# Modulation vectors made during the two layers: products on the vector engine, sums over the partitions on the tensor engine

## The chip, the cores and the metric

The kernel runs on one core of one Trainium2 chip. The metric is device time in microseconds (us) of one execution, as the median of several runs. The engines that matter here are TensorE (PE in the profile, its weight loads PEld), VectorE (DVE), ScalarE (ACT), GpSimd (POOL) and SyncE (SP), which issues the DMAs that load weights.

## What is computed

Two blocks of a network on 512 latent tokens and 256 context tokens, 1024 features, float32. The first block has two attention layers. Each layer is modulated by vectors that are products of a conditioning vector with a weight matrix; so is each layer of the second block:

```python
def layer(x, cx, c_silu, cctx_silu, norm_w, ada_w, ada_b, ..., need_ctx):
    mod = c_silu @ ada_w + ada_b                  # [3 * 1024]
    mod_c = cctx_silu @ ada_w + ada_b
    shift, scale, gate = jnp.split(mod, 3, axis=-1)
    shift_c, scale_c, gate_c = jnp.split(mod_c, 3, axis=-1)
    hx = rmsnorm(x, norm_w) * (1 + scale[:, None, :]) + shift[:, None, :]
    hc = rmsnorm(cx, norm_w) * (1 + scale_c) + shift_c
    ...                                           # projections, three attentions, output projection
    x = x + gate[:, None, :] * (ux @ w_out)

def _adaln(cvec, w_mod, b_mod, n_chunks):         # second block, six vectors of 1024 per layer
    m = jax.nn.silu(cvec) @ w_mod[:, :n_chunks * D_MODEL] + b_mod[:n_chunks * D_MODEL]
    return [m[:, None, j * D_MODEL:(j + 1) * D_MODEL] for j in range(n_chunks)]
```

The second layer of the first block has no further use for the context tokens, so it needs no gate for them. The second block needs the context's vectors only for the first two of its first layer's six chunks.

## The kernel before

The program is written with a scheduling library: the Python code issues instructions in one order, and a scheduler sorts them for each engine by priority and readiness; each engine then works through its own queue in that order. Stages follow one another. In a first phase (up to about 181 us in the profile) the modulation vectors of layer 0, the filters and the context's recurrence are made. Then come the two layers, `layer(0, ...)` and `layer(1, ...)`, up to about 1600 us; then the second block with a mixer, an expert mixture, a conformer and another expert mixture.

In a layer the projections (`proj_tok`, `proj_feat`) load 256 columns of weights with two tiles of a ring (`wload`, L123; tiles of 4 KB per partition, four in the ring during the layers), split them into two parts on ScalarE (L153) and GpSimd (L154), and multiply them with the tokens in three products each (L159 to L161 or L327 to L329). Attention works on pairs of heads between them: row maxima on VectorE (L671 to L692), transposed scores and products with v on TensorE (L721, L724, L727), exponentials on ScalarE (L777). In the layers PSUM's eight banks are divided as m=2, s=2, av=1, b=3, and any other kind, such as "a", takes from b.

At the end of each projection `self.fill(1)` (L331, L356) runs one unit of a generator, `self.filler`, set up at L400 to L404. Its units make modulation vectors that are needed later: 12 units for layer 1 of the first block (3 x 1024 columns of `ada_w[1]`), 16 for chunks 2 to 5 of the second block's first layer, and 12 for chunks 0 to 2 of its second. A unit's instructions get the same priorities as the code that follows it (`background`, L164).

A unit of `adaln` (L191) takes 256 columns: two ring tiles of weights [128, 4, 256], then eight matmuls (L205) with a stationary of 32 columns, 128 rows each, in which the two vectors silu(c) and silu(c_ctx) stand at a unit's own column pair and the rest is zero, and 256 moving weight columns. Four of them share TensorE's columns at a time. A matmul in float32 has two records in the profile. VectorE then adds the product to a tile of rows (`adr`, L208, L210). After every twelve units (or the last) two matmuls with the selection matrix `sel` (L215) sum and transpose the rows, and VectorE adds the bias (L218). The zero-padded vectors `z1` and `z2` come from `cvec` (L178), at the start of the first block. The first phase uses `adaln` for layer 0's vectors and the first eight groups of `w_mod[0]`, the conformer for the last twelve of `w_mod[1]` (L1555).

Of the kernel before, what the change touches and what calls it, by code (L numbers as in the profile page):

```python
# [43 lines left out]
def kview(src):  # L44
    """[k * 128, n] of DRAM as [128, k, n]."""
    return src.rearrange("(k p) n -> p k n", p=128)


class K:
# [20 lines left out]
    def chunks(self, pool, tag, n, width, dt=F32, bufs=None):  # L70
        """n tiles of their own, so that each waits only for what held its place."""
        return [self.t(pool, [128, width], dt, tag=f"{tag}{i}", bufs=bufs) for i in range(n)]

    @contextmanager
    def banks(self, **caps):
        """A phase's division of the eight PSUM banks among kinds of use; any other kind takes from b."""
# [35 lines left out]
    # ------------------------------------------------------------------ streamed weights  # L112
# [10 lines left out]
    def wload(self, src, nk, n, tag="ring", size=1024, bufs=None):  # L123
        """Weights [128, nk, n], loaded through 4 KB tiles of the ring; w(k, m) is a view of chunks k..k+m."""
# [17 lines left out]
    def split(self, src):  # L142
        """Exact two-part float32r split of src ([128, <= 512] elements)."""
# [20 lines left out]
    def background(self, offset=0):  # L164
        """Instructions that give way to those of the code that follows."""
# [11 lines left out]
    # ------------------------------------------------------------------ modulation vectors  # L177
    def cvec(self, pool, name):  # L178
        """Zero-padded stationary columns of silu(c), silu(c_ctx)."""
# [9 lines left out]
        return z  # L189

    def adaln(self, z, wsrc, ncols, bias, mod, tmp, part=None):  # L191
        """mod[128, ncols / 128, 2] = (silu(c), silu(c_ctx)) @ w + b with features on partitions; a
        generator of units, one 256-column group each.  Row 2g + v of a group's product is vector v."""
# [31 lines left out]
    # ------------------------------------------------------------------ norms  # L225
# [3 lines left out]
    def sums(self, n, tmp, square=True, sc=None, kind="q", four=True, alloc=None):  # L229
        """Sums over the features: add(k, x) takes chunk k as soon as it is there (four: four of them share the  # L230
        tensor engine); add() gives four partial sums of 32 equal rows each, SBUF [128, n]."""
# [34 lines left out]
    def rsqrt(self, tmp, x):  # L266
        """1 / sqrt(x) for x > 0, [128, <= 24], by Newton's method from an estimate out of the exponent."""
# [10 lines left out]
    def tokmean(self, s, n, tmp):  # L278
        """Means per token, tokens on partitions: [128, n / 128] in PSUM."""
# [5 lines left out]
    def spread(self, r, n):  # L285
        """[128 tokens, n / 128] to [128 rows, n tokens], every row the same; in PSUM."""
# [1696 lines left out]
```

## Time and profile before

| what | us |
|---|---|
| median of 3 runs | 3200.13 |
| lowest and highest | 3197.77, 3202.67 |
| span of the profiled execution, first to last instruction | 3197.7 |
| PE busy | 2936.5 (92%) |
| DVE busy | 1390.3 (43%) |
| ACT busy | 932.1 (29%) |
| POOL busy | 782.0 (24%) |

The profiled execution's time and its span can be taken as one; it lies 2.4 us below the median of the runs. Busy time is the union of an engine's instructions; matmuls overlap in the pipeline, so that the mean duration of one times the count is more than the busy time. "The chain of waits" is the chain of work that ended last, followed back from the last instruction to what released it at each step; a line's share of it is time that the end waited for. "issue" is time in which an engine waited for nothing that the profile shows. A fraction such as 0.98 for PEclk is the granted clock of TensorE, the mean over a window of its two levels (2.4 GHz, and half of that).

### The profile page before, as it was taken

The page shows a single profiled execution, that of the slowest core. Times are in us where ns is not written, and L with a number is a line of the kernel's source. Part 1 is how long each engine was busy: PE and PEld are TensorE (multiplying, and loading weights), DVE is VectorE, ACT ScalarE, POOL GpSimd, SP SyncE. Part 2 cuts the span into 40 slices and gives each one's busy share as a digit, 9 for nine tenths or more (in the row PEclk, how much of TensorE's full clock was granted, in tenths as well). Part 3 has the DMA queues.
Part 4 walks back from the last instruction along what each step waited for, and adds up shares of the span by engine and source line. Part 5 has one row for each costly group of instructions (what it writes and reads, how often), then busy time and mean ns, then how long its engine had stood idle before and what let it go on. Part 6 is the DMA issues. An engine that isn't in the chain of part 4 may idle for free.

```text
span 3197.7 us, 39095 instructions
## 1 busy us (share of the span) xinstructions
PE 2936.5 (92%) x15406; PEld 1837.9 (57%) x15406; DVE 1390.3 (43%) x2645; ACT 932.1 (29%) x1667; POOL 782.0 (24%) x669
## 2 busy tenths in 40 slices
PE   6899999999898999999998779999899998899988
PEld 3485567765677566755775664444444664444443
DVE  5765553455405543675267761111215552211122
ACT  3434543354313444343345220100012231001001
POOL 2233232322423333343444640000002430000000
PEclk8999999999999999999999889999999998999999
DMA  9631133211533133322331268999993567999993
GB/s 286 198 113 34 34 122 110 79 63 43 171 99 113 47 99 116 123 65 94 112 97 60 92 261 344 385 391 401 399 362 90 163 228 282 393 387 394 397 404 122
DMA packets 302599, 621.36 MB, mean 194 GB/s; under 512 B 15215, under 2 KB 185207, under 8 KB 302160
## 3 DMA queue, kind: packets, MB, share of 16 engines
q1 hardware_dynamic: 294240, 597.63, 51.4%
q0 software_dynamic: 4848, 17.04, 1.7%
q10 hardware_dynamic: 3328, 4.20, 0.4%
q8 instruction: 121, 1.98, 0.2%
q14 instruction: 62, 0.51, 0.1%
HBM read 603.96 MB, written 14.95 MB: 194 GB/s over the span
## 4 chain that ended last, share of the span: by engine, by line
PE 77%; DVE 13%; ACT 3%; issue 3%; POOL 2%; DMA 2%; SPq 0%; DVEq 0%; ACTq 0%; POOLq 0%
PE b L1793 22%; PE b L159 8%; PE b L160 7%; PE b L161 7%; PE av L727 5%; PE b L1744 5%; PE b L205 3%; PE s L721 3%; DVE xn L1772 2%; PE s L724 2%; PE m L702 1%; PE b L329 1%; PE b L328 1%; PE b L327 1%; PE b L1771 1%
## 5 line engine op out<-in xcount | busy, mean ns | idle before, releaser
L154 POOL TENSOR_TENSOR wl<-ring,wh 128x512 fp32r<-128x512 f32 x304 | 404.4, 1333 | 715.7 <-ACT wh L153 702.8
L1793 PE MATMUL b<-mr,xs 128*64 128x512 f32 x1920 | 441.2, 604 | 0.0
L153 ACT CAST wh<-ring 128x512 fp32r<-128x512 f32 x304 | 186.8, 618 | 548.8 <-PE b L161 393.4
L159 PE MATMUL b<-hh,wh 128*128 128x512 f32 (+1 forms) x800 | 293.2, 367 | 2.4 <-DVE sc L585 1.1
L160 PE MATMUL b<-hh,wl 128*128 128x512 f32 (+1 forms) x800 | 290.3, 363 | 1.3 <-POOL wl L154 1.3
L161 PE MATMUL b<-hl,wh 128*128 128x512 f32 (+1 forms) x800 | 288.7, 362 | 0.1
L1793 PEld LDWEIGHTS b<-mr,xs 128*64 128x64 f32 x1920 | 143.4, 139 | 225.2 <-issue 215.3
L1793 PE MATMUL b<-mq,xs 128*64 128x512 f32 x1152 | 260.8, 599 | 0.0
L1744 PEld LDWEIGHTS b<-G,kt 128*128 128x128 f32 x1024 | 137.7, 211 | 136.1 <-issue 80.6
L1744 PE MATMUL b<-G,kt 128*128 128x128 f32 x1024 | 160.2, 308 | 52.0 <-DVE G L1736 52.0
L727 PE MATMUL av<-P,kv 128*64 128x512 f32 (+2 forms) x672 | 187.2, 514 | 2.8 <-ACT P L777 1.8
L159 PEld LDWEIGHTS b<-hh,wh 128*128 128x128 f32 x800 | 151.7, 190 | 37.4 <-issue 8.2
L160 PEld LDWEIGHTS b<-hh,wl 128*128 128x128 f32 x800 | 152.3, 190 | 30.9 <-issue 8.7
L161 PEld LDWEIGHTS b<-hl,wh 128*128 128x128 f32 x800 | 151.5, 189 | 29.0 <-issue 8.4
L1749 DVE TENSOR_SCALAR xs<-b,s1m,m 128x128 f32<-128x128 f32 x64 | 26.2, 410 | 322.2 <-PE b L1744 322.2
L1793 PEld LDWEIGHTS b<-mq,xs 128*64 128x64 f32 x1152 | 85.9, 137 | 138.2 <-issue 133.2
L777 ACT ACTIVATE P<-s 128x512 f32<-128x512 f32 (+2 forms) x224 | 116.9, 550 | 114.2 <-PE s L724 111.0
L327 PE MATMUL b<-wh,hh 128*128 128x256 f32 x512 | 147.8, 289 | 2.3 <-DVE kb L1124 1.3
L329 PE MATMUL b<-wh,hl 128*128 128x256 f32 x512 | 147.5, 289 | 1.1 <-DVE hl L310 0.9
L328 PE MATMUL b<-wl,hh 128*128 128x256 f32 x512 | 147.4, 288 | 0.3 <-POOL wl L154 0.3
L1747 ACT ACTIVATE xs<-b,m,s1m 128x128 f32<-128x128 f32 x64 | 29.3, 457 | 373.4 <-PE b L1744 373.4
L1553 POOL TENSOR_SCALAR dg<-ident,vec 128x128 f32<-128x128 f32 x5 | 2.9, 595 | 537.1 <-PE b L1793 537.1
(536 smaller groups left out, 5588.0 us busy)
## 6 DMA issues: line engine op xcount, KB each, us to landing
mr<-in_exp_w_dram SPq DMA_DIRECT2D x240, 1024.0 KB, 9.7
mq<-in_exp_w_dram SPq DMA_DIRECT2D x144, 1024.0 KB, 11.5
ring<-in_w_mod_dram SPq DMA_DIRECT2D x96, 512.0 KB, 4.0
ring<-in_w_in_dram SPq DMA_DIRECT2D x96, 512.0 KB, 3.5
ring<-in_ada_w_dram SPq DMA_DIRECT2D x48, 512.0 KB, 3.6
ring<-in_w_out_dram SPq DMA_DIRECT2D x32, 512.0 KB, 4.1
bias<-in_BS_dram POOLq DMA_DIRECT2D x16, 512.0 KB, 4.0
bias<-in_BT_dram POOLq DMA_DIRECT2D x16, 512.0 KB, 4.1
```

The lines of the kernel that those rows point to most:

```text
L153: nc.scalar.copy(h, src)
L154: nc.gpsimd.tensor_tensor(l, src, h.bitcast(F32), op=ALU.subtract)
L159: m(out, w[0], x[0], start=start, stop=False, skip_group_check=chk)
L160: m(out, w[1], x[0], start=False, stop=False, skip_group_check=chk)
L161: m(out, w[0], x[1], start=False, stop=stop, skip_group_check=chk)
L327: m(o, hh, wh[:, kk, :], start=(k == 0 and i % 2 == 0), stop=False, skip_group_check=True)
L328: m(o, hh, wl[:, kk, :], start=False, stop=False, skip_group_check=True)
L329: m(o, hl, wh[:, kk, :], start=False, stop=stop, skip_group_check=True)
L727: mm(av[64 * i:64 * i + 64, a:b], vf(i, kt), P, start=start, stop=stop)
L777: nc.scalar.activation(p[:, :w], ps[:, :w], AF.Exp)
L1744: mm(px, kt[t][:, c * 128:c * 128 + 128], G[:, t, :], start=t == 0, stop=t == 3)
L1793: mm(ps[hf][64 * e:64 * e + 64, :], lhs(k, e), wt[e][:, k2, hf * 512:hf * 512 + 512], start=k == 0, stop=k == 7)
```

## The change

`adaln_v` takes the place of `adaln` in the filler of the two layers. The product runs on VectorE: a tile of weights [128 rows, n columns] is multiplied by one number per partition, silu(c) of that row, and added to a running sum `acc` (tag `adr`, [128, 1024], one buffer). With both vectors (`nv=2`) n is 512 and a group has 16 such operations in two units; with one vector (`nv=1`) n is 1024 and a group has 8 operations in four units. At a group's end eight matmuls sum over the partitions: 128 columns of `acc` are the stationary operand, two columns of ones are moving. Then VectorE adds the bias. The number of units, the ring tiles per unit and the bytes loaded stay the same; the rows that a load fetches are 512 or 1024 elements long in place of 256. Vectors that are not used (the context's gate of layer 1, the context's part in the second block's later chunks) are no longer made.

`cvec` also returns the vectors without padding, kept in the pool of the first block, and the padded ones move to a pool of the first phase; the two calls come after the loads of sink, rope and bsel. The first phase and the conformer keep `adaln`. Comments and docstrings are dropped throughout, which shifts line numbers only.

```diff
-    def cvec(self, pool, name):
+    def cvec(self, pool, name, keep=None):
...
-        return z
+        if keep is None:
+            return z
+        s = self.t(keep, [128, 8, 2], tag=name + "s")
+        nc.vector.tensor_copy(s[:], z[:, :, 32:34])
+        return z, s
...
+    def adaln_v(self, z, wsrc, a, b, nv, bias, mod, tmp):
+        nc = self.nc
+        n = 1024 // nv
+        for c0 in range(a, b, n):
+            acc = self.t(tmp, [128, 1024], tag="adr", bufs=1)[:].rearrange("p (v n) -> p v n", v=nv)
+            for k0 in range(0, 8, 2 * nv):
+                w = self.wload(kview(wsrc[k0 * 128:(k0 + 2 * nv) * 128, c0:c0 + n]), 2 * nv, n)
+                for k in range(2 * nv):
+                    for v in range(nv):
+                        x = z[:, k0 + k, v:v + 1]
+                        if k0 + k == 0:
+                            nc.vector.tensor_scalar(acc[:, v, :], w(k), x, None, op0=ALU.mult)
+                        else:
+                            nc.vector.scalar_tensor_tensor(acc[:, v, :], w(k), x, acc[:, v, :], op0=ALU.mult, op1=ALU.add)
+                if k0 + 2 * nv < 8:
+                    yield 1
+            ps = self.bank("a")
+            m = n // 128
+            for c in range(m):
+                for v in range(nv):
+                    o = 2 * (nv * c + v)
+                    nc.tensor.matmul(ps[:, o:o + 2], acc[:, v, c * 128:c * 128 + 128], self.one32[:, 0:2], start=True, stop=True)
+            c0 //= 128
+            nc.vector.tensor_tensor(
+                mod[:, c0:c0 + m, 0:nv], ps[:, 0:2 * nv * m].rearrange("p (c v two) -> p c v two", v=nv, two=2)[:, :, :, 0],
+                bias[:, c0:c0 + m][:, :, None].to_broadcast([128, m, nv]), op=ALU.add)
+            yield 1
...
-            z1 = self.cvec(fp, "cv1")
-            z2 = self.cvec(fp, "cv2")
             self.sink = load("sink", [128, 2, 8])
...
                 with self.pool("fl") as fl, self.pool("ec") as ec:
+                    z1, c1 = self.cvec(ec, "cv1", fp)
+                    z2, c2 = self.cvec(ec, "cv2", fp)
...
             def units():
-                yield from self.adaln(z1, A["ada_w"][1], 3 * D, self.v("ada_b1"), self.mods[1], fp)
-                yield from self.adaln(z2, A["w_mod"][0], 6 * D, self.v("b_mod0"), self.m2[0], fp, (8, 24))
-                yield from self.adaln(z2, A["w_mod"][1], 6 * D, self.v("b_mod1"), self.m2[1], fp, (0, 12))
+                yield from self.adaln_v(c1, A["ada_w"][1], 0, 2 * D, 2, self.v("ada_b1"), self.mods[1], fp)
+                yield from self.adaln_v(c1, A["ada_w"][1], 2 * D, 3 * D, 1, self.v("ada_b1"), self.mods[1], fp)
+                yield from self.adaln_v(c2, A["w_mod"][0], 2 * D, 6 * D, 1, self.v("b_mod0"), self.m2[0], fp)
+                yield from self.adaln_v(c2, A["w_mod"][1], 0, 3 * D, 1, self.v("b_mod1"), self.m2[1], fp)
```

## Rows read from the trace of the kernel before

**Rows 1.** Busy time by engine in the layers' stretch, with its header.

```profile
core 0: us, PE busy (x) PEld busy (x) DVE busy (x) ACT busy (x) POOL busy (x), PEclk, DMA share, GB/s
181.00:1600.00 1419.00, 1367.06 (x7656) 950.74 (x7654) 698.09 (x1411) 562.17 (x1033) 490.40 (x456) 0.98 0.28 90
```

**Rows 2.** The chain of waits in the same stretch, by line.

```profile
by line: PE av L727 12.1%; PE b L159 11.5%; PE b L160 11.2%; PE b L161 11.1%; PE s L721 5.7%; PE b L205 4.4%; PE s L724 4.3%; PE m L702 3.2%; issue 2.9%; PE b L329 2.7%; PE b L328 2.6%; PE b L327 2.6%; PE m L684 1.4%; PE m L689 1.3%; PE m L
```

**Rows 3.** The same stretch, instructions of L205 alone: PE, PEld, clock, DMA.

```profile
181.00:1600.00 1419.00, 90.11 (x640) 25.70 (x640) 0.98 0.28 90
```

**Rows 4.** Windows of 15 us, columns of rows 1.

```profile
200.00:215.00 15.00, 11.34 (x103) 10.55 (x102) 13.95 (x30) 7.79 (x18) 6.52 (x6) 1.00 0.40 126
215.00:230.00 15.00, 12.83 (x76) 12.12 (x77) 9.89 (x25) 4.12 (x7) 3.92 (x4) 0.77 0.12 36
298.00:313.00 15.00, 13.62 (x87) 10.64 (x79) 13.47 (x30) 4.57 (x12) 6.59 (x6) 1.00 0.34 105
975.00:990.00 15.00, 13.38 (x100) 12.27 (x99) 14.98 (x28) 8.24 (x15) 0.37 (x1) 0.95 0.01 1
1333.00:1348.00 15.00, 15.00 (x137) 12.93 (x129) 13.07 (x38) 6.05 (x15) 8.80 (x11) 1.00 0.34 106
1348.00:1363.00 15.00, 14.04 (x65) 10.11 (x66) 14.51 (x31) 6.84 (x15) 7.44 (x8) 1.00 0.44 141
1363.00:1378.00 15.00, 12.31 (x77) 8.63 (x70) 14.51 (x22) 4.52 (x8) 5.84 (x6) 0.89 0.47 147
```

**Rows 5.** Timeline: start, length, engine, line; L205 among transposes and a unit alone.

```profile
641.21 0.62 PE L205 MATMUL b<-ring,cv2z 128*32 128x256 f32 x2
688.11 1.07 PE L205 MATMUL b<-ring,cv2z 128*32 128x256 f32 x16
```

**Rows 6.** Tile of the rows (adr) in the layers: durations min/median/max, and who waited.

```profile
L210 DVE TENSOR_TENSOR adr<-adr,b x36: 355/420/429, 201.1 to 1514.0; 128x256 f32<-128x256 f32 x36
L215 PE MATMUL b<-sel,adr x16: 192/276/401, 588.2 to 1514.8; 128*128 128x32 f32 x16
  PE b L215: 4.8, 2
  PEld b L159: 2.7, 4
  PE b L159: 1.3, 2
```

**Rows 7.** Timeline: eight records, two moving columns, in the second block.

```profile
1946.30 1.05 PE L1756 MATMUL b<-pr,G 128*128 128x2 f32 x8
```

**Rows 8.** Two VectorE lines of two SBUF inputs: count, min/median/max ns.

```profile
L586 DVE TENSOR_TENSOR y<-sc,y x24: 630/692/1785, 400.2 to 1514.3; 128x512 f32<-128x512 f32 x24
L1432 DVE TENSOR_TENSOR t<-t,t x4: 1204/1204/1207, 1777.1 to 1852.7; 128x1024 f32<-128x1024 f32 x4
```

**Rows 9.** Timeline of GpSimd and VectorE around 140 us; that line over the run.

```profile
139.84 1.27 POOL L1106 TENSOR_TENSOR ol<-fs,oh 128x512 fp32r<-128x512 f32 x1 [8.44 <-ACT oh L1105]
140.10 1.03 DVE L273 TENSOR_TENSOR nww<-nwy 128x2 f32<-128x2 f32 x1
L273 DVE TENSOR_TENSOR nww<-nwy x51: 152/164/1261, 31.8 to 3186.1; 128x4 f32<-128x4 f32 x21, 128x2 f32<-128x2 f32 x9, 128x12 f32<-128x12 f32 x6, 128x24 f32<-128x24 f32 x6
```

**Rows 10.** L205 alone in the first and the last of six windows: PE, PEld.

```profile
200.00:215.00 15.00, 1.07 (x16) 0.42 (x16) 1.00 0.40 126
1363.00:1378.00 15.00, 3.54 (x16) 0.81 (x16) 0.89 0.47 147
```

**Rows 11.** Waits of SP's queue in the layers: total, times, longest.

```profile
SPq L134 <- PE b L205: 218.7, 45, 29.4
```

**Rows 12.** Timeline of the start: loads issued on SP, first unit's second half.

```profile
2.12 0.91 SPq L182 DMA_DIRECT2D cv<-in_cv_dram  x2
4.06 0.43 SPq L368 DMA_DIRECT2D bsel<-in_bsel_dram  x1
10.70 1.08 PE L205 MATMUL a<-ring,cv2z 128*32 128x256 f32 x8 [0.90 <-DMA ring<-in_w_mod_dram]
```

## What the change does to the time: the prediction

> **What bounds the kernel now.** The change touches the stretch between the first phase and the second block, 181 to 1600 us of the profile: the two layers. I read first the busy times of that stretch [rows 1]: of 1419 us TensorE is busy 1367 at a mean granted clock of 0.98, VectorE 698, GpSimd 490, and the DMA share is 0.28. So TensorE is full, VectorE is idle half of the time, and loads are cheap. Next the chain of waits in the same stretch, by line [rows 2]: the products of the modulation vectors (L205) are 4.4% of it, 62.4 us, although they bring nothing that the next instruction of a layer needs. The same line alone is busy 90.1 us there [rows 3]; its chain share is 0.69 of that. The rest filled time in which TensorE waited anyway. Last the windows where VectorE is the full one [rows 4]: six of 15 us in which it is busy 13 us or more, 90 us in all, 6.3% of the stretch. Outside of them added VectorE work has idle time to go to; inside it has little (TensorE is full too in one of the six, so 90 us is rather too much).
>
> **Removed.** 40 units of 8 matmuls, two records each: 640 records [rows 3]. A unit alone takes 1.07 us for its 16 records; between transposes of another tile shape two records take 0.62 us [rows 5]. That is why the mean of a unit is 90.1 / 40 = 2.25 us, and why the chain share is the term to use: 62.4 us. The four selections of L215 go too (16 records, 0.28 us at the median [rows 6]), 3.2 us busy if each stood alone, of which I count 2. PSUM: before, each of the 40 units takes a "b" bank and holds it until VectorE has added it to the rows; afterwards 12 banks are taken. TensorE's waits on those adds ahead of L159 are 2.7 + 1.3 us [rows 6]; I count 2 as gone. Removed from the path: 62.4 + 2 + 2 = 66.4 us.
>
> **Added on TensorE.** The weights of layer 1 come in 4 groups of 512 columns for both vectors and 1 of 1024 for one, the second block's in 4 and 3 of 1024 for one: 12 groups. Each ends with eight matmuls of a 128 x 128 stationary and two moving columns: 96 matmuls, 192 records. The same form stands in L1756, eight records in 1.05 us, 0.131 each [rows 7]: 25.2 us. At the chain share of the work that it replaces, 0.69, that is 17.4 us, which I take, because the eight become ready together and can run in a row. Bounds: nothing at all (they fall into TensorE's gaps) to 0.31 each, the price of L205's records among others [rows 5], 59.5 us, or 41 at that share.
>
> **Handoffs.** Each group has to wait for its sum on VectorE, and TensorE's queue is in order: a projection's matmuls stand behind a waiting one. Before, the four selections waited 4.8 us in two of four cases [rows 6], 1.2 us on average. Twelve handoffs cost 0 (the sum is long done) to 14.4 us; I take 6, because the new ones come at the end of whole groups of units and not of one late addition.
>
> **Added on VectorE.** 64 operations of 128 x 512 and 64 of 128 x 1024. Rows of the same width with two SBUF inputs take 0.692 and 1.204 us [rows 8]: 44.3 + 77.1 = 121.4 us (the 16 that start a sum have one input and may be cheaper). The additions to the rows go: 36 of 0.42 us [rows 6] and four first copies, 40 x 0.42 = 16.8 us. Then the meeting with GpSimd. A product of 128 x 2 whose median is 0.164 us took 1.03 us and ended with GpSimd's 1.27 us tensor operation [rows 9]; the 128 x 512 product at L586 has a median of 0.692 and a maximum of 1.785 us [rows 8], so a meeting costs up to 1.09 us. GpSimd is busy 490 of 1419 us [rows 1], 0.35. With 112 two-input operations, each met with that chance and paying half: 112 x 0.35 x 0.55 = 21 us. VectorE's new work is 121.4 + 21 = 142 us, net 126.
>
> The Trainium skill says of this, in GPSIMD Engine Reference, section 1 (Specifications), that GpSimd's SBUF interfaces are shared with VectorE and contended by VectorE instructions with two SBUF inputs. By that rule nearly all of the added operations are of the contended kind, which speaks against the change; the row of the 128 x 2 product agrees.
>
> **How much of it is on the path.** If it falls evenly, 6.3% of 142, 9 us. If it falls where the units stand now, six of the 40 begin in the six VectorE-bound windows (first and last shown [rows 10]): the two early ones carry eight 512-wide operations each, 5.5 us, the four later ones two of 1024, 2.4 us: 20.7 us. I take the middle, 15, because VectorE can also do the sums earlier, as soon as the weights are there, but its queue is in order and the head norm's and rope's short steps stand behind them. Its lower bound is 0, the upper 35 (20.7 with every operation meeting GpSimd at the half price).
>
> **Clock.** After the VectorE-bound stretch at 200 us the granted clock is 0.77 over 15 us [rows 4]: 3.4 us lost. L205 runs in several of these waits; without it TensorE idles more there. I count one more such drop, 3.4 us, between 0 and 12.
>
> **At nothing.** The bytes are the same: two ring tiles of 512 KB per unit, 40 units, in rows of 2 or 4 KB in place of 1 KB; the DMA share of 0.28 hides them [rows 1]. What changes is who frees the tile: SP waits 218.7 us in 45 times for L205 to free one [rows 11], and other loads stand behind it; now VectorE frees it. A unit's VectorE time is at most 5.5 us, against a spacing of 1419 / 40 = 35 us between units; if VectorE came late by a whole spacing, the next projection's weights would be late, which is part of the slow rival below. The two small loads of the first phase move behind sink, rope and bsel on SP's queue (issued at 2.12 us before, the last of the three at 4.06 [rows 12]): up to 1.4 us later, while the second half of the first unit waits for its weights until 10.70 us [rows 12]. If that cover were gone, 1.4 us. The two copies that keep the short vectors are covered the same way.
>
> **Sum.** -66.4 + 17.4 + 6 + 15 + 3.4 = -24.6 us. Against the profiled execution, 3197.7 us, that gives 3173.1; the median of the runs lies 2.4 us above that execution: **3175.5 us**, 0.8% faster. With the bounds: -66.4 alone is 3134; -66.4 + 41 + 14.4 + 35 + 12 = +36.
>
> **Rivals.**
> 1. More is freed than the chain says: the 28 us of L205 off the chain (90.1 - 62.4) let other TensorE work move up. Then the saving is the busy time, 90.1 + 3.2 - 25.2 = 68 us, less some 8 of VectorE: 3140 us. For it: TensorE is busy 96% of the stretch, so hardly a gap is free. Against: the chain counts that time as waiting for others.
> 2. A wait takes the place of the products: the 96 small matmuls land between other shapes at 0.31 us (41 us on the path) and each group waits for its sum (14.4), with 12 for VectorE and 3 for the clock: -66.4 + 70 = +4, 3204 us. For it: L205 itself is interleaved now [rows 5]. Against: a group's eight have no input of their own to wait for once the sum is there.
> 3. The slower one: VectorE becomes the bound, at one place, its in-order queue. Sums stand ahead of the short steps that TensorE waits for (row maxima, the splits of q and k, head norm and rope). VectorE's foreground work fills 698 / 1419 = 0.49 of the time [rows 1]. If a sum delays the foreground whenever the two meet, half of 142 us is exposed, 70 us: -66.4 + 17.4 + 6 + 70 + 3 = +30, 3230 us. It decides from 40 us exposed, 28% of the new work. For it: 60% busy engines make others wait. Against: TensorE's 1367 of 1419 us busy leave 52 us for all of its waits now, most of them in the six windows' kind of stretch.
> 4. It does not shorten the path, because L205 only fills gaps. Then the 62.4 is fiction, and only added work counts. The chain speaks against it; it ends within the prices of 2 and is counted there.
>
> **How the numbers follow.** Chances: forecast 0.54 (own range 3152 to 3190), rival 1 0.16, rivals 2 and 4 together 0.14, rival 3 0.16. The range reaches from rival 1 with all in its favour, 3130, to rival 2's end, 3207; above it lies most of rival 3, below it next to nothing. A measurement of this kernel can tell about 0.2%, 6.4 us. Faster by more: 0.54 + 0.16 + 0.05 of rival 2 = 0.75; within: 0.09; slower: 0.16.
>
> **What would show it.** Right: no L205 in 181 to 1600 us, a line of matmuls with two moving columns with 192 records and about 25 us busy there, VectorE about 820 us busy, TensorE about 1300, the layers' end some 25 us earlier and everything after it unchanged. The VectorE term is wrong if the six windows have grown by more than 20 us; the handoff term, if the waits of the two-column matmuls on the sums exceed 15 us; the clock term, if the stretch's granted clock falls below 0.97. The forecast as a whole is wrong if TensorE's waits for VectorE grow by more than 40 us, or if ring loads land after VectorE asked for them.

## The result, and the profile after

The changed kernel takes 3163.05 us (median of four runs, 3156.76 to 3166.45) against 3199.26 (3197.77 to 3202.67): a ratio of 0.9883, 95% interval 0.9872 to 0.9895, 36 us faster. Forecast were 3175.5 us, own range 3152 to 3190, 24.6 us faster: the sign was right and the largest term nearly so, the gain came out 12 us larger. One more set of four runs gave 3163.43 (0.9888). Two executions of the same kernel differ by some us at one stage: the layers ended 35 us earlier than before in one profile and 40 in the other, so stage times below carry about 5 us.

The profile's busy line, then the layers' stretch (it ends 35 us earlier, hence 1565), with the columns of rows 1:

```profile
PE 2887.3 (91%) x14942; PEld 1846.0 (58%) x14942; DVE 1503.0 (48%) x2743; ACT 930.1 (29%) x1667; POOL 799.7 (25%) x669
```

```profile
181.00:1565.00 1384.00, 1319.25 (x7190) 957.13 (x7188) 804.91 (x1502) 560.20 (x1033) 504.39 (x456) 0.96 0.29 92
```

```profile
181.00:1560.00 1379.00, 1312.47 (x7180) 952.25 (x7178) 801.34 (x1497) 558.46 (x1029) 503.32 (x456) 0.97 0.29 92
```

The last fence is the second profile of the same kernel. Against rows 1, TensorE's busy time fell by 47.8 us (1367.06 to 1319.25) and its idle time (length minus busy) rose by 12.8 (51.9 to 64.8). The granted clock fell from 0.98 to 0.96, in the second profile to 0.97. VectorE does 107 us more. The chain of waits, followed back from the end, breaks off at 1576 us in this profile, so rows 2 have no counterpart.

The clock is lower in every execution, and not in the profiled ones alone: over the whole program the mean granted clock is 0.949 to 0.953 in the eight runs of the changed kernel, and 0.955 to 0.960 in the runs of the kernel before.

The new work, by the tile of the sums (columns as in rows 6: min/median/max ns, first and last start; then who waited):

```profile
L253 PE MATMUL b<-one,adr x192: 164/252/374, 198.8 to 1476.5; 128*128 128x2 f32 x192
L245 DVE SCALAR_TENSOR_TENSOR adr<-ring,cv1s,adr x57: 648/741/2271, 179.8 to 530.3; 128x512 f32<-128x512 f32 x50, 128x1024 f32<-128x1024 f32 x7
L245 DVE SCALAR_TENSOR_TENSOR adr<-ring,cv2s,adr x49: 1266/1284/2154, 587.8 to 1400.0; 128x1024 f32<-128x1024 f32 x49
L243 DVE TENSOR_SCALAR adr<-ring,cv1s x7: 473/478/1171, 200.8 to 470.0; 128x512 f32<-128x512 f32 x6, 128x1024 f32<-128x1024 f32 x1
L243 DVE TENSOR_SCALAR adr<-ring,cv2s x7: 743/752/1243, 586.0 to 1347.7; 128x1024 f32<-128x1024 f32 x7
  DMA ring<-in_w_mod_dram: 61.4, 17
  DMA ring<-in_ada_w_dram: 6.7, 4
  DVE mod L255: 5.4, 3
  DVE m L255: 3.3, 4
  PEld m L738: 0.4, 1
  PEld m L865: 0.4, 1
```

(The two DMA lines are what VectorE waited for ahead of these operations, the last four lines are who waited for them.) No product of `adaln` (L205 before, L209 now) stands in the layers. 192 records of L253 are there, and VectorE's sums are busy 134 us: L245 123.2 and L243 10.8; eight of the 128 operations stand ahead of 181 us. Only two weight loads of TensorE wait for anything of this tile, 0.8 us in all, both for L245. VectorE in its turn waits 8.7 us for L253, ahead of the bias (L255). What L253 itself waited for stands in the groups of lines (busy, mean ns of one, then the idle time before them and what ended it):

```profile
L253 PEld LDWEIGHTS b<-one,adr 128*128 128x128 f32 x192 | 28.3, 214 | 4.2 <-DVE sc L621 1.8 <-issue 1.6 <-ACT raw L1007 0.2
L253 PE MATMUL b<-one,adr 128*128 128x2 f32 x192 | 26.3, 254 | 0.6 <-DVE sc L621 0.5
```

It never waited for a sum of L245. VectorE waited 68 us for weights (61.4 and 6.7), 48.5 of it in the output projection of layer 0, where TensorE idled 4 us in all.

Now by stage: attention of layer 0, its output projection, attention of layer 1, its output projection. Each line covers the same work before and after:

```profile
180.00:820.00 640.00, 613.49 (x3612) 423.85 (x3614) 341.15 (x700) 267.58 (x511) 200.93 (x197) 0.98 0.23 72
820.00:973.00 153.00, 147.21 (x813) 114.57 (x805) 30.65 (x63) 35.70 (x61) 51.68 (x38) 0.96 0.44 147
973.00:1475.00 502.00, 488.79 (x2751) 335.39 (x2751) 285.27 (x594) 215.30 (x387) 184.51 (x180) 0.99 0.30 94
1475.00:1600.00 125.00, 118.57 (x494) 77.92 (x493) 41.02 (x57) 44.07 (x75) 53.28 (x41) 0.96 0.31 100
```

```profile
180.00:826.00 646.00, 607.09 (x3443) 434.43 (x3441) 404.55 (x763) 267.24 (x511) 207.21 (x198) 0.95 0.23 73
826.00:960.00 134.00, 129.87 (x736) 110.63 (x737) 46.22 (x73) 35.55 (x61) 56.15 (x38) 0.97 0.52 165
960.00:1440.00 480.00, 465.08 (x2533) 333.76 (x2532) 313.57 (x612) 213.74 (x386) 187.22 (x179) 0.98 0.30 96
1440.00:1565.00 125.00, 118.21 (x491) 79.31 (x489) 41.57 (x58) 44.30 (x77) 54.40 (x42) 0.96 0.31 98
```

Layer 0's attention, in which 18 of the 40 units are issued, became 6 us longer (640 to 646). The output projection with what follows up to layer 1's heads saved 19 us (153 to 134), layer 1's attention 22 (502 to 480), its output projection, in which one unit stood before and after only the last eight small matmuls, nothing (125 and 125). From there to the end the shift of every instruction stays at 35 us. In layer 0's attention TensorE's idle time went from 26.5 to 38.9 us and its clock from 0.98 to 0.95; length times the missing share of the clock is 13 and 32 us. So some 31 us more were lost there, all that the removed work gave and 6 more.

How they were lost begins at 205 us. First VectorE (start, length, line; some lines between are left out), then GpSimd, TensorE, and the two windows that rows 4 begin with:

```profile
206.27 0.18 DVE L308 TENSOR_TENSOR nww<-nwy 128x24 f32<-128x24 f32 x1
206.94 0.94 DVE L309 SCALAR_TENSOR_TENSOR nww<-ss,nww 128x24 f32<-128x24 f32 x1
207.81 1.83 DVE L245 SCALAR_TENSOR_TENSOR adr<-ring,cv1s,adr 128x512 f32<-128x512 f32 x1
209.56 0.17 DVE L310 SCALAR_TENSOR_TENSOR nwy<-nww,nwy 128x24 f32<-128x24 f32 x1
210.41 0.74 DVE L245 SCALAR_TENSOR_TENSOR adr<-ring,cv1s,adr 128x512 f32<-128x512 f32 x1
211.07 0.17 DVE L309 SCALAR_TENSOR_TENSOR nww<-ss,nww 128x24 f32<-128x24 f32 x1
211.16 1.78 DVE L245 SCALAR_TENSOR_TENSOR adr<-ring,cv1s,adr 128x512 f32<-128x512 f32 x1
212.87 0.17 DVE L310 SCALAR_TENSOR_TENSOR nwy<-nww,nwy 128x24 f32<-128x24 f32 x1
```

```profile
206.56 2.53 POOL L154 TENSOR_TENSOR wl<-ring,wh 128x512 fp32r<-128x512 f32 x2 [6.36 <-ACT wh L153]
210.78 1.62 POOL L154 TENSOR_TENSOR wl<-ring,wh 128x512 fp32r<-128x512 f32 x1 [1.69 <-ACT wh L153]
```

```profile
221.60 0.45 PE L907 MATMUL m<-ident,raw 128*128 128x128 f32 x1 [6.44 <-DVE raw L897]
```

```profile
200.00:215.00 15.00, 15.00 (x127) 14.95 (x127) 14.57 (x34) 8.22 (x18) 4.58 (x5) 1.00 0.35 108
215.00:230.00 15.00, 8.19 (x46) 7.09 (x45) 13.67 (x29) 3.49 (x7) 7.19 (x7) 0.77 0.26 83
```

L306 to L310 are the Newton steps of the head norm, each needing the one before: 0.17 us of work where nothing disturbs them, and here a sum of 0.74 or 1.8 us stands between one and the next. TensorE's L907, the transpose of what the head norm makes, waits 6.44 us (5.8 before). Little is lost there yet: the two windows together have TensorE busy 23.19 us, in place of 24.17 [rows 4], at the same clock. While the head norm was late, TensorE ran matmuls of a projection that are due later: from 180 us to the instruction that stood at 245 us before, it ran 25 each of L159 to L161, in place of 10 or 11. It lacks them from 336 us on. The same stretch before, after, and in a run that has no unit at the head norm (e6 below), then one of five such waits in the kernel after:

```profile
330.00:400.00 70.00, 69.49 (x344) 40.84 (x343) 35.07 (x61) 37.23 (x73) 20.02 (x17) 1.00 0.08 25
336.00:407.00 71.00, 63.50 (x279) 32.78 (x277) 35.43 (x64) 36.24 (x71) 17.49 (x15) 0.93 0.03 8
326.00:395.00 69.00, 65.98 (x317) 37.24 (x316) 34.97 (x61) 36.78 (x72) 20.13 (x17) 1.00 0.05 16
```

```profile
371.19 0.68 PE L706 MATMUL m<-k,q1l 128*128 128x512 f32 x1 [0.94 <-DVE mp L707]
```

Before, 31 or 32 each of L159 to L161 ran here between the scores (L706, which is L670 before) and the row maxima on VectorE (L707, L671 before); after, 8 or 9 are left. L706 now waits for the row maxima 3.1 us in five times, before not once, although no sum stands in VectorE's queue from 362 to 384 us. Idle time is 7.5 us in place of 0.5, and the clock 0.93 in place of 1.00, another 5 us of 71. So the place where a sum delays VectorE and the place where the time is lost lie some 150 us apart. In the profiles of all runs below that have sums at the head norm, the 71 us that end where 400 us was before hold 6.6 to 7.9 us of idle time and a clock of 0.80 to 0.93; in those that have none there, at most 3.3 us and 0.98 to 1.00.

The other dear stretch is the last, from 700 us on: before, after, and without the multiply-adds (e1 below).

```profile
700.00:820.00 120.00, 107.53 (x555) 63.45 (x558) 69.22 (x134) 52.84 (x103) 31.38 (x31) 0.95 0.12 40
700.00:826.00 126.00, 108.98 (x525) 65.61 (x523) 73.80 (x136) 51.60 (x102) 30.78 (x30) 0.86 0.14 45
688.00:808.00 120.00, 107.11 (x528) 64.28 (x526) 68.68 (x133) 50.13 (x100) 31.62 (x31) 0.90 0.14 46
```

Idle time is 17.0 us in place of 12.5, and the clock 0.86 in place of 0.95; but it is 0.92 in the second profile of the changed kernel, and 0.90 without the multiply-adds, so what the sums do to the clock here is not told apart from scatter.

### The profile page after: what moved, and what is told of

Read it like the earlier page. It is cut to its first block, busy times and chain, and to the rows that moved or that the text cites. A ratio compares the mean times of both kernels' runs of the same rounds, so it can differ in the third digit from the quotient of the medians.

```text
span 3162.7 us, 38266 instructions
## 1 busy us (share of the span) xinstructions
PE 2887.3 (91%) x14942; PEld 1846.0 (58%) x14942; DVE 1503.0 (48%) x2743; ACT 930.1 (29%) x1667; POOL 799.7 (25%) x669
## 5 line engine op out<-in xcount | busy, mean ns | idle before, releaser
L154 POOL TENSOR_TENSOR wl<-ring,wh 128x512 fp32r<-128x512 f32 x304 | 418.2, 1379 | 655.0 <-ACT wh L153 636.9
L159 PE MATMUL b<-hh,wh 128*128 128x512 f32 (+1 forms) x800 | 295.8, 371 | 3.0 <-DVE sc L621 3.0
L161 PE MATMUL b<-hl,wh 128*128 128x512 f32 (+1 forms) x800 | 290.6, 365 | 0.1
L763 PE MATMUL av<-P,kv 128*64 128x512 f32 (+2 forms) x672 | 193.8, 522 | 2.9 <-ACT P L813 1.7
L159 PEld LDWEIGHTS b<-hh,wh 128*128 128x128 f32 x800 | 154.1, 193 | 32.3 <-issue 5.6
L161 PEld LDWEIGHTS b<-hl,wh 128*128 128x128 f32 x800 | 153.4, 192 | 25.1 <-issue 4.5
L1855 DVE SCALAR_TENSOR_TENSOR yl<-b,gh,xs 128x512 fp32r<-128x512 f32 x32 | 22.6, 746 | 247.2 <-ACT xs L1854 247.2
```

Source lines behind the costliest of these rows:

```text
L154: nc.gpsimd.tensor_tensor(l, src, h.bitcast(F32), op=ALU.subtract)
L159: m(out, w[0], x[0], start=start, stop=False, skip_group_check=chk)
L161: m(out, w[0], x[1], start=False, stop=stop, skip_group_check=chk)
L763: mm(av[64 * i:64 * i + 64, a:b], vf(i, kt), P, start=start, stop=stop)
```

## The experiments

All were measured beside the kernel before on the same chip. A letter names a theory within its own quote: V and Q put the loss on VectorE's queue; P stands for another theory from the moved units on (the place of the units) than in the runs before them.

**Without the multiply-adds.**

```diff
-                            nc.vector.scalar_tensor_tensor(acc[:, v, :], w(k), x, acc[:, v, :], ...)
```

> Leaves out all 112 multiply-adds of the sums, so that only the first product of each sum is made and the modulation vectors are incomplete; loads, small matmuls and the order of units stay. Theory V (the sums on VectorE hold up the layers' own steps in layer 0, TensorE then waits and its granted clock falls: 112 us of the layers at half clock after the change, 68 before, and 12 us more idle): these losses go, some 22 + 12 us, 3130 us. Rival P (the clock falls because L205's products no longer fill TensorE's waits; VectorE's sums are hidden): the losses stay, 3158 us.

3143.33 us (3142.04 to 3148.69), ratio 0.983 [0.9815, 0.9845], about midway between V's number and P's. The 112 operations cost 20 us of the changed kernel. The layers' line (its own end is 1543):

```profile
181.00:1543.00 1362.00, 1307.59 (x7171) 946.79 (x7169) 695.25 (x1388) 558.42 (x1025) 490.05 (x456) 0.97 0.30 93
```

Of the 22 us by which the stretch is shorter than after's, 10 are idle time of TensorE (64.8 to 54.4) and the other 12 busy time (1319.25 to 1307.59), with the clock at 0.97 in place of 0.96. Against the second profile of after it is 17 us, 12 idle and 5 busy. As far as two digits tell, the clock does not come back to the 0.98 of before, though next to nothing is added on VectorE; but two profiles of one kernel differ by as much. By stage, nearly all of the 20 us stand in layer 0's attention (627 us without the multiply-adds, 646 with them), 12 of them ahead of 600 us, by the shift of the same instructions; layer 1's attention has 475 and 480.

**Both: the products back on TensorE as well.**

```diff
                 w = self.wload(kview(...), 2 * nv, n)
+                pp = self.bank("a")
+                for i in range(8):
+                    j, per = i % 4, n // 256
+                    nc.tensor.matmul(pp[32 * j:32 * j + 32, :256], self.one32[:], w(i // per)[:, ...256 columns], start=i < 4, stop=i >= 4)
```

> The changed kernel with eight products per unit put back on TensorE, of the same size and tile shape as L205's, on the same weight tiles, with ones as the stationary operand; their result is not used. The sums on VectorE stay. Theory V: TensorE gets its 62 us on the path back and VectorE's losses stay, 3163 + 62 = 3225 us. Rival P: the products fill the waits again and the clock recovers, 3163 + 62 - 22 = 3203 us.

3231.85 us (3228.86 to 3237.72), 1.0106 [1.0091, 1.0121]. Against the changed kernel the products cost 69 us. The layers, then the products alone in the same stretch (PE, PEld, clock):

```profile
181.00:1638.00 1457.00, 1392.05 (x7795) 978.40 (x7793) 795.07 (x1498) 558.62 (x1024) 502.79 (x456) 0.96 0.28 88
```

```profile
181.00:1638.00 1457.00, 77.68 (x624) 24.51 (x624) 0.96 0.28 88
```

They are busy 77.7 us, so 0.89 of their busy time reaches the end, against the 0.69 that the chain gave; of the 90.1 us that L205 was busy, the same 69 us would be 0.77. The clock is 0.96 as in after: putting the products back did not raise it, which speaks against a clock that fell because they are missing. With before and the run above this makes a square: products alone 3200, sums alone 3163, both 3232, neither 3143. (Before also has the additions to the rows and lacks the small matmuls.)

**One small matmul in place of eight.**

```diff
-            for c in range(m):
-                for v in range(nv): ...
-                    nc.tensor.matmul(ps[:, o:o + 2], acc[:, v, c * 128:c * 128 + 128], self.one32[:, 0:2], ...)
+            nc.tensor.matmul(ps[:, 0:16], acc[:, 0, 0:128], self.one32[:, 0:16], start=True, stop=True)
```

> Leaves out seven of the eight small matmuls at each of the 12 sums' ends (one with 16 moving columns is left), so that most elements of the vectors are wrong. The prediction priced all 96 at 25.2 us busy and 17.4 us on the path, so 84 of them at 15 us: 3148 us. If they stand between matmuls of other shapes at 0.31 us a record: 36 us, 3127 us. If they fall into TensorE's gaps: 3163 us.

3152.94 us (3146.68 to 3155.35), 0.9851 [0.9836, 0.9865]. The 84 matmuls that are gone cost 10 us, so the 96 some 11.5, under half of their 26.3 busy us; medians of four runs tell this to a few us.

**Layer 1's vectors back on TensorE.**

```diff
-                yield from self.adaln_v(c1, A["ada_w"][1], 0, 2 * D, 2, ...)
-                yield from self.adaln_v(c1, A["ada_w"][1], 2 * D, 3 * D, 1, ...)
+                yield from self.adaln(y1, A["ada_w"][1], 3 * D, ..., (0, 12), 6, 10)
```

> The 12 units of the first block's layer 1 go back to TensorE (with the selection after six units in place of twelve, for lack of memory); the 28 units of the second block keep their sums on VectorE. The two traces stand level when the 12 units are over (shift about 0 us at 600 us), so by an even account these units bring nothing: 3163 us. If the 512-wide sums of these units (8 operations per unit) are what costs VectorE's time, theory V in its narrow form: the loss of layer 0 goes, 3145 us. Rival P: 12 units of L205 back on the path at 19 us, 3175 us.

(The edit also makes the padded vectors that this needs.) 3175.42 us (3174.02 to 3178.9), 0.9931 [0.9914, 0.9947]: 12 us slower than the changed kernel, P's number, and V's narrow form fell. Eight of the twelve units are the ones with two vectors and 512 columns, and all stand in the crowded stretch; putting them back gained nothing in all. By the rates of the runs above, twelve units of products cost 12 x 69 / 40 = 21 us and the 40 small matmuls that go give back 5; so by this account the sums that go were worth some 4 us of the 20, with 49 us less VectorE work in the layers. The trace says otherwise. This kernel loses 5 us of its own ahead of 600 us, where its units are those of before: its instructions stand 4 us later at 600 us than in the kernel before, and 1 us earlier at 200; the early selection (L219) waits 2.9 us there. The twelve units' sums are the 12 us that the run without multiply-adds gains by 600 us.

**The second block's vectors back on TensorE.**

```diff
-                yield from self.adaln_v(c2, A["w_mod"][0], 2 * D, 6 * D, 1, ...)
-                yield from self.adaln_v(c2, A["w_mod"][1], 0, 3 * D, 1, ...)
+                yield from self.adaln(y2, A["w_mod"][0], 6 * D, ..., (8, 24), 6, 10)
+                yield from self.adaln(y2, A["w_mod"][1], 6 * D, ..., (0, 12), 6, 10)
```

> The mirror of the kernel before this one: sums on VectorE for the 12 units of layer 1 only, the 28 units of the second block on TensorE as before. Even account: 3199 us, the time before. Theory V in its narrow form: the loss of layer 0 without the later gain, 3199 + 18 = 3217 us. Rival P: 3199 - 12 = 3187 us.

3206.67 us (3200.14 to 3209.78), 1.0019 [1.0008, 1.0029]: the twelve units alone gain nothing, they lose 6 us. By the same rates 28 units of products cost 48 us and 56 small matmuls give back 7; the difference to the changed kernel is 44, so by this account these sums were worth nothing that shows. The number lies between the even account's and V's. The two halves give 25 and -6 us, 19 together, where the whole gives 36. Both mixed kernels select after six units in place of twelve, and both hold the waits of the two ways. At 600 us, when the twelve units are over, this run stands 1.6 us later than the kernel before, as the changed kernel does (0.9); it loses another 6 us by 960 us, where its units run on TensorE as before. With the 5 us of the other half, 11 of the missing 17 us are the mixed kernels' own; the rest was not settled.

**No unit at four crowded projections.**

```diff
     def fill(self, n):
+        self.nf += self.filler is not None
+        if self.nf in (3, 4, 17, 18):
+            return
```

> The changed kernel with no unit issued at the 3rd, 4th, 17th and 18th projection of layer 0, so that no sums stand between the steps of the first head norm (200 to 235 us) and in the last attention group (740 to 760 us); the units move back and the last four come in the output projection of layer 1. Nothing is left out. Theory V (place decides what a sum costs): without sums the trace stands 8 us earlier at 240 us and another 7 us between 720 and 800; 15 us less, 3148 us. Rival S (any other order of the queues moves the time by chance, places mean nothing): 3163 us within 8.

3157.31 us (3156.5 to 3157.84), 0.9867 [0.9852, 0.9882]. By 800 us the instructions stand some 15 us earlier than before, where after stands 6 us later: 21 us (15 in the second pair of profiles), with four units fewer done by then. That is V's direction, but the time itself lies within S's range, so this run alone does not decide; part of the gain is lost again. The last four units now stand in layer 1's output projection and cost 4 us there, and the second block, untouched, scatters by 5.

**All units 200 priorities later.**

```diff
-        with self.background():
+        with self.background(200):
```

> The units get a priority 200 instructions later than the code around them, so that the scheduler takes them only where nothing else is ready. In VectorE's queue the sums of the third unit still stand between the dependent steps of the head norm. Theory V: no gain there, 3163 us within 5. Rival: that the sums cost time because they are taken ahead of the layers' own steps; then 12 to 20 us of the sums' cost go, 3147 us.

3187.18 us (3184.39 to 3191.49), 0.9958 [0.9941, 0.9974], 24 slower than the changed kernel; neither number came up. Of these 24 us, 12 are there at 1600 us (layer 0 at 400 us stands 21 us later than before); another 13 come in the conformer, whose own filler goes through the same function and was put off as well. So half of this run says nothing of the layers. In VectorE's queue the sums of the third unit still stand between the head norm's steps: a lower priority did not take them out of the way, and the run doesn't tell what such a place would be worth.

**Every multiply-add twice.**

```diff
                             nc.vector.scalar_tensor_tensor(acc[:, v, :], w(k), x, acc[:, v, :], ...)
+                            nc.vector.scalar_tensor_tensor(acc[:, v, :], w(k), x, acc[:, v, :], ...)
```

> Every multiply-add of the sums is done twice, in the same place and on the same data (112 more VectorE operations of 128 x 512 or 128 x 1024; the vectors come out nearly doubled, which the rest of the program carries through in the same time). Nothing else changes: loads, small matmuls and their places are those of the changed kernel. It tells whether the 20 us that the sums cost (the run without them) are a fixed share of their VectorE time, or the foot of a steeper curve. Theory L (linear: they cost about 0.15 of their busy time, some of it as half clock): another 129 us of VectorE work, another 20 us, 3183 us. Theory Q (rival 3 of the prediction, VectorE's in-order queue: a share that grows as VectorE fills, half of the work exposed once it is met): 50 to 65 us more, 3213 to 3228, with VectorE's busy share of the layers going from 0.58 to 0.67. Under L the half-clock time grows by some 20 us, under Q TensorE's waits for VectorE do, above all in layer 0's attention.

3229.06 us (3227.33 to 3230.93), 1.0096 [1.0081, 1.0111]: 66 us slower than the changed kernel. Just above Q's numbers. By VectorE's busy time in the layers, the first copy adds 110 us (695.25 without multiply-adds, 804.91 with them) and costs 20, a share of 0.18; the second adds 122 (to 926.71) and costs 66, 0.54. VectorE waits 76 us for weights in place of 68, and TensorE for none, so late weights are not the reason. The second copy stands behind the first in the same places, so the run tells nothing of sums spread over other places. The stretch as a whole (it ends at 1630), and the four stages:

```profile
181.00:1630.00 1449.00, 1344.98 (x7219) 972.93 (x7219) 926.71 (x1607) 561.54 (x1034) 526.35 (x460) 0.94 0.28 88
```

```profile
180.00:856.00 676.00, 621.70 (x3463) 442.65 (x3463) 465.03 (x829) 267.42 (x511) 220.79 (x201) 0.93 0.23 71
856.00:998.00 142.00, 131.20 (x732) 111.49 (x732) 59.78 (x76) 35.83 (x61) 57.04 (x38) 0.94 0.48 156
998.00:1506.00 508.00, 479.13 (x2564) 345.55 (x2565) 361.24 (x649) 216.02 (x389) 199.05 (x183) 0.96 0.30 93
1506.00:1630.00 124.00, 112.95 (x462) 73.24 (x460) 40.66 (x57) 42.26 (x73) 50.46 (x39) 0.96 0.29 89
```

Idle time of TensorE is 104 us against 64.8, and its clock 0.94. Attention of layer 0 is 30 us longer than after's, attention of layer 1 28: there the first dose had cost 5 us (475 and 480, above), the second costs as much as in layer 0.

**The four units moved to layer 0's output projection.**

```diff
+        if self.nf in (3, 4, 17, 18):
+            return
+        if self.nf in (19, 20, 21, 22):
+            n = 2
```

> As the run without units at the 3rd, 4th, 17th and 18th projection of layer 0, but the four units so left over do not move to the end of layer 1: the four projections after that (19th to 22nd call, the first of layer 0's output projection) run two units each, so that the last units stand where the changed kernel has them. Theory P (place: what a sum costs depends on whether VectorE's foreground has idle time there; in layer 0's output projection VectorE is busy 25 to 38% and TensorE idles not at all): the layers keep what the earlier run gained by 960 us (29 us against 13 for the changed kernel) and lose nothing in layer 1's output projection; 4 to 6 us better than that run, 3151 to 3153 us. Theory W (weights: VectorE already waits 61 us there for the units' loads, and twice the units ask for twice the bytes through the same four ring tiles): the output projection's own weights come late, some 5 us for each of the four, and the gain goes: 3165 to 3177 us.

3155.95 us (3151.92 to 3159.11), 0.9864 [0.9847, 0.9881]. The median is 3 us above P's number and far below W's.

**The three side by side,** the changed kernel and the two edits above once more.

> The changed kernel itself, on the same chip and in the same rounds as the two versions that follow, so that differences of a few us can be told. Theory P (place): 3163 us, as measured already; the two versions that follow lie 6 to 8 us below it and within 2 us of each other. Theory N (their gain was the scatter of four runs, since the intervals overlap): all three within 3 us of one another.

> No unit at the 3rd, 4th, 17th and 18th projection of layer 0, as in the run before. P: 3157 us, 6 below the changed kernel. N: 3160 to 3163.

> The same, with the four units made up at the 19th to 22nd call, as in the run before. P: 3155 to 3156 us, 7 below the changed kernel. N: 3160 to 3163.

Medians 3163.43, 3161.39 and 3151.85; ratios 0.9888 [0.9873, 0.9902], 0.9872 [0.9857, 0.9886], 0.9853 [0.9837, 0.987]. N fell for the moved units, whose interval lies below the changed kernel's; skipping alone is 2 us below the changed kernel here, as N has it, and not the 6 of P. With the four runs of each from earlier, some of them on other chips, medians of eight are 3163.4, 3157.8 and 3153.2. So the moved units are worth about 10 us over the changed kernel (every one of its eight runs, 3150.7 to 3159.1, lies under all but one of the changed kernel's, 3156.8 to 3168.5); skipping alone lies between. Of the versions that leave nothing out the moved one is the fastest. Its stages, in the last of these runs:

```profile
180.00:806.00 626.00, 595.21 (x3420) 426.41 (x3418) 390.19 (x752) 265.99 (x511) 202.78 (x197) 0.97 0.21 68
806.00:948.00 142.00, 132.71 (x748) 113.06 (x748) 57.58 (x78) 36.09 (x62) 56.91 (x38) 0.94 0.58 188
948.00:1428.00 480.00, 464.32 (x2534) 333.36 (x2535) 315.06 (x617) 213.67 (x386) 187.36 (x179) 0.98 0.30 96
1428.00:1553.00 125.00, 118.39 (x491) 79.24 (x490) 41.90 (x58) 44.31 (x77) 54.66 (x42) 0.96 0.31 97
```

Layer 0's attention is 626 us, in place of 646 with all units and 640 before, at 30.8 us idle and a clock of 0.97. The output projection is 142 us: it gave back 8 of those 20 us, with 9.3 us idle in place of 4.1 and a clock of 0.94 in place of 0.97. VectorE is busy only 58 of 142 us there and the loads run at 188 GB/s in place of 165; whether late weights (W, at a small size) or the sums do it was not told apart. Layer 1 is as in after.

## Why the forecast came out as it did

**The products: 66.4 us forecast, 69 measured.** The term was the chain's 62.4 us plus 4. The run with both shows 69 us for the products alone, without selections and additions. The chain's share was too low: 0.77 to 0.89 of the products' busy time reaches the end, not 0.69, as rival 1 said in direction. The 4 us for selections and additions, which no run measured, hide most of that. By busy times, the lines removed were 90.1 [rows 3] and at most 3.2 us, L253 is 26.3, so 67 us of work went, while TensorE's busy time fell by only 47.8. By this account the other 19 us are slower matmuls, at the lower clock; it is an estimate, as a line's matmuls overlap with those of others.

**The small matmuls: 17.4 forecast, about 11.5 measured.** Their busy time was right (25.2 against 26.3). The step that was off is the share: 0.69 was taken from the work that they replace, and it was about 0.44. Why so little of them reaches the end was not shown.

**Handoffs: 6 forecast, next to 0 in the trace.** TensorE's matmuls wait for no sum; two weight loads wait 0.8 us for L245. The 8.7 us that VectorE waits for L253 had no term, and no run prices them. This 6 and the 6 of the line before, with 3 of the products, are the larger gain.

**Sums on VectorE and clock: 15 + 3.4 forecast, 20 measured for the multiply-adds.** The size of VectorE's work was close (142 forecast, 134 busy in the layers for 120 of the 128 operations), and the total too, but what it was made of was not. The forecast put most on waits and let the clock lose one drop. Idle time of TensorE rose by 12.8 us, and the granted clock of the whole stretch fell to 0.96 (second profile 0.97): by length times missing share that is 55 (41) us in place of 28, 13 to 27 more, beyond the upper bound of 12. The profile's figure is rounded to 0.01, 14 us of this stretch. Over the whole program it has three digits, 0.957 before and 0.949 (0.952) after: 161 (152) us missing in place of 138, 14 to 24 more. That is an upper measure, as a low clock in idle time costs nothing; the work account above gives 19. So the clock term is the mis-sized one, 3.4 against some 14 to 24, and the forecast's own sign for it, a stretch below 0.97, came up in one profile of two. That 20 lies near the 18.4 of the two terms is luck: the multiply-adds' idle time came out below the 15 (10 or 12 us), and the clock made up for it (12 or 5 us of slower matmuls).

Taken together: -69 + 11.5 + 0 + 20 = -37.5 us, against 36 us of gain measured.

**The place.** The middle between "evenly" and "where the units stand" was the wrong picture of where. Layer 0's attention lost all it had been given (6 us longer), all later stages kept theirs. The six windows of rows 4 were the wrong unit: four of them lie after 970 us, in layer 1, where the sums cost 5 us, and one large loss of layer 0 arises in the first window but falls at 336 to 407 us, where VectorE is busy half of the time. It comes by the order of TensorE's work, which the forecast had no term for. Leaving four of layer 0's eighteen places empty gave back 15 to 21 us there.

**GpSimd.** Half the price at each meeting, 21 us in all, was forecast. The 128 x 512 multiply-add has a median of 0.741 us and a maximum of 1.828 (the 2.271 above is one of 128 x 1024). The two long ones above ended 0.55 us after GpSimd's L154 did (206.56 + 2.53 = 209.09, and 207.81 + 1.83 = 209.64; 212.40 and 212.94); beyond 0.74 us each of them stood. All eleven of that size that took over 1 us ended 0.54 or 0.55 us after a GpSimd tensor operation that ran when they began, and all nineteen of 128 x 1024 that took over 1.3 us ended 1.08 or 1.09 us after one; those during which GpSimd's operation began lost nothing. This is the rule of the Trainium skill that the forecast weighed (GPSIMD Engine Reference, section 1), and the trace agrees. Beyond their medians the 112 took 17 us in all, close to the 21. L243, with one SBUF input, is held as well: its two long ones of 128 x 512 (0.88 and 1.171 us over a median of 0.478) ended 0.28 us after a GpSimd operation. It goes the other way too: an L154 that began 0.1 us into a row of six multiply-adds took 5.11 us, where others take 1.28.

**The rivals.** Rival 1 let all busy time come free, 68 us net of the small matmuls; measured are 57.5 (69 - 11.5), about midway between it and the forecast's 49, and it had the wrong price for VectorE (8 in place of 20). Rival 2 fell: neither the handoffs nor the interleaved price came up. Rival 3 fell for this change, but the size that it gave is real: the double dose costs 66 us for 122 us of work, the half that the prediction gave it. That it is VectorE's queue that costs it is likely and not shown step by step: TensorE's waits grow for row maxima, head norm and the rest alike. Its point, 40 us exposed, was not reached at 20. What the forecast lacked is that the share is not fixed: 0.18 for the first dose, 0.54 for the second.

**At nothing.** One of the forecast's signs of being wrong as a whole came up: ring loads landed after VectorE asked for them, and it waited 68 us. The sign was too strict, as little of it reached TensorE: in the stage with 48.5 us of these waits it idled 4.1 us (5.8 before). The other sign, TensorE's waits for VectorE growing by over 40 us, did not come up: all its idle time grew by 12.8. The moved small loads and copies cost nothing that shows: the instructions around 160 us stand 0.4 us earlier. The bytes hid as forecast, with SP's queue waiting 202 us for L243 and L245 to free a ring tile in place of 218.7 us for L205 [rows 11]:

```profile
SPq L134 <- DVE adr L245: 150.1, 50, 28.8
SPq L134 <- DVE adr L243: 51.6, 8, 8.4
```

**What stays open.** Whether the clock without the multiply-adds is below 0.98 by more than two profiles differ, what costs the other 7 of the 19 us in layer 0's attention (12 stand ahead of 600 us), why the second dose is so much dearer in layer 1 than the first, and 6 of the 17 us by which the two halves of the change together give less than the whole.

## What to carry to other kernels

When work goes from a full engine to one that is half idle, its price is no fixed share: here 0.18 of the first 110 us reached the end, and 0.54 of the next 122, so a measured double dose tells more than the mean busy share. Look for chains of short dependent steps on the receiving engine, and keep the new work out of these by giving it to a stage where that engine idles; four of forty units moved were worth 10 us. Look for the loss further on as well: the full engine may fill a delay with work that it lacks later. Count the granted clock of the full engine over the whole stretch, not one drop: of the 71 us at the row maxima 7 went to idle time and 5 to the clock.

## What was not expected of the hardware

The granted clock over 180 to 826 us fell from 0.98 to 0.95 with 12 us more of idle time in 646, and to 0.93 in the double dose with 54 us idle in 676. A VectorE multiply-add that began while GpSimd ran a tensor operation ended 0.55 us (128 x 512) or 1.08 us (128 x 1024) past that operation's end, in all thirty cases that took longer than usual. The same kernel's two profiles differ by 5 us in the layers, at 0.96 and 0.97 of granted clock.
